# The shift's weights from POOL's queue, begun within the scale's stage, and the input transposes spread over three groups of sums

## The chip, the cores and the metric

The kernel runs on one core of one Trainium2 chip. The metric is the device time of one execution in microseconds (us), lower is better. The engines are TensorE (PE; its weight loads have a row of their own, PEld), VectorE (DVE), ScalarE (ACT), GpSimd (POOL) and SyncE (SP). SP and POOL issue the transfers spoken of here, and 16 DMA engines carry them.

## What is computed

One layer of an encoder step: a layer norm whose result is scaled and shifted by columns that come from a small vector `c`, one wide input projection, four mixer branches (state space, attention, mLSTM, convolution), an output projection and a last norm. The change lies in the first line and a half:

```
shift, scale, gate = jnp.split(c.astype(jnp.float32) @ w_mod + b_mod, 3, axis=-1)
u = layer_norm(x) * (1.0 + scale[:, None]) + shift[:, None]
# then: proj = u @ w_in, split into the inputs of the four branches
```

There are 1024 prompt rows (worked on in two halves) and 32 sample rows; the model width is 2048, which is 16 blocks `k` of 128.

## The kernel before

**Number format.** Each projection is done as three products of split operands: `u = uh + ul` and `w = wh + wl`, with matmuls `uh*wh`, `ul*wh`, `uh*wl`. The shift is not added to `uh` and `ul`; instead, each `uh`/`ul` tile has two spare columns (0 and 1) that hold the shift, and a column tile of the projection that has these columns gets its bias from them.

**The scale's stage**, `startup()` (L1384 to L1467). `load_norm` loads five row tiles of `x` (four of 128 rows, one with the 32 sample rows) and normalises them on ACT (L275). `quads(g)` brings 16 weight tiles of group g of the scale (`wmr`, 256 KB each, L1420, issued by SP) into the pool IO, which has 20 tiles, and adds them up on PE in four steps of four matmuls (L208), here called quads. With four groups there are 16 quads. After the fourth quad of a group `mod_columns` copies the sum (`mr`, DVE, L231), transposes it (`modc`, PE, L233), reduces it and writes four scale columns (DVE, L236 and L240). With these `build_u0(k)` builds four blocks of `u`: five transposes on PE (L297 and L299, here one set, tile `xt`), the scaling on ACT (L301), the split on DVE (L302, L304) and POOL (L303, 32 columns). `parts_of(g)` are four parts of 12 matmuls each (L1437 to L1439), which multiply the blocks of group g for two column tiles, "gates", that need no shift. PE's order is written out by hand (`inorder`): the parts of group g-1 stand between the builds of group g.

**The shift's stage.** Two more gate tiles (L362 to L364) are woven with `mod_group(g, 0)`, the same sums for the shift's columns: 64 loads, issued by SP at L217, one load or one quad at a time at 64 places. `shift_columns` (POOL, L287 and L288) writes the spare columns, and the first column tile with a shift follows. Weights of the column tiles are loaded by SP as well (L333).

`behind(a, b)` makes instruction a stand after b in the order, without a wait.

Of the kernel before, what the change touches and what calls it, by code (L numbers as in the profile page):

```python
# [13 lines left out]
P = 128  # L14
# [48 lines left out]
def step_kernel(ctx, tc, xp, xs, cst, wmss, wmg, bgate, win, wsm, wout, lng, lnb, ck, cv,  # L63
# [136 lines left out]
    inorder = tc.keep_in_program_order  # L200
    begun = [None]
# [9 lines left out]
    def mod_group(g, part):  # L211
        o = ZT("mod")
        for kq in range(4):
            ws = []
            for i in range(4):
                wr = IO("wmr")
                nc.sync.dma_start(wr[:, 0:512], wmss[g, 4 * kq + i, part])  # L217
                ws.append(wr)
                if i < 3:
                    yield 1  # L220
# [30 lines left out]
    def load_norm(src, rows, keep):  # L251

        tiles = []
        for q in range(4):
            if keep and q < 3:
                t = up.tile([P, 546], F32, tag=("uh", "ul")[(len(keep) + q) % 2], name=nm("x"))
            else:
                t = (IO if keep else WK)("x")
# [12 lines left out]
        if keep:  # L271
            nb = SM(1, "bnb", 3)
            V.scalar_tensor_tensor(nb[:rows], mv[:rows, 0:1], -1.0, rs[:rows], op0=ALU.mult, op1=ALU.mult)
            for q in range(4):
                A.activation(tiles[q][:rows, 0:512], tiles[q][:rows, 0:512], AF.Identity, bias=nb[:rows],  # L275
                             scale=rs[:rows])
# [13 lines left out]
    def build_u0(xts, k):  # L290

        uh, ul = new_u(0, k)
        uf = WK("uf")
        q, o = divmod(k, 4)
        pt = ST("xt")
# [4 lines left out]
        for pp, n, c0, j in ((pt, 512, 0, 0), (pt2, SMP, 512, 1)):  # L300
            A.activation(uf[:, c0:c0 + n], pp[:, 0:n], AF.Copy, scale=scale1[:, k, j:j + 1])  # L301
        V.tensor_copy(uh[:, 2:546], uf[:, 0:544])  # L302
        return (G.tensor_tensor(ul[:, 514:546], uf[:, 512:544], uh[:, 514:546].bitcast(F32), op=ALU.subtract),  # L303
                V.tensor_tensor(ul[:, 2:514], uf[:, 0:512], uh[:, 2:514].bitcast(F32), op=ALU.subtract))  # L304
# [1081 lines left out]

    def startup():
# [58 lines left out]

        m = quads(0)
        for _ in range(3):  # L1450
            next(m)
        for g in range(4):
            o = next(m)
            m = quads(g + 1) if g < 3 else iter(())
            p = parts_of(g - 1) if g else iter(())
            next(p, None)
            mod_columns(g, 1, o, inorder)
            for i in range(4):
                if i < 3:
                    next(p, None)  # L1460
                begun[1:] = build_u0(xts, 4 * g + i)
                if i < 3:
                    next(m, None)
        for _ in parts_of(3):
            pass
        for x in range(2):
            keep_gate(x, [(acc[x][i][:, 0:n], t0, n) for i, (_, t0, _, n) in enumerate(sp_)])  # L1467

    startup()
    for i in begun:  # L1470
# [36 lines left out]
    def chain(*gs):  # L1507
        for g in gs:
            yield from g

# [23 lines left out]
    for h in range(2):  # L1534
# [7 lines left out]
        if h == 0:  # L1542
            weave([(stage1(b_gate(p)), 2) for p in range(2, 4)], [(chain(*[mod_group(g, 0) for g in range(4)]), 64)])
# [126 lines left out]
```

## Time and profile before

| what | us |
|---|---|
| median of 3 runs (1965.37 to 1971.18) | 1969.03 |
| the profiled execution | 1967.32 |
| its span on the core | 1965.3 |
| PE busy within the span | 1885.7 (96%) |
| start to the first quad | 21.26 |
| the scale's stage, from there to the first matmul of L362 | 72.5 |
| from there to the first shifted column tile | 81.1 |

All times of rows are from the start of the span. A row of a timeline gives the start, the time to the end of the last of its instructions, the engine, the line, the operation with its tiles (out<-in, partitions x elements), how many instructions run on without a gap (every matmul of 32-bit operands at L208, L233 and L297 is recorded in two passes in some rows, so that a quad is x8), and in brackets the idle time ahead and what ended it. The distance from one row's start to the next row's start is the time that PE's order spends on the row. In the rows by stretch, each engine has its busy time and the number of its instructions; PEclk is the clock that PE was granted (1.00 is 2.4 GHz, 0.50 is 1.2 GHz), and behind it are the busy share of the DMA engines and what they moved. No record of the clock exists ahead of 37.7 us, so the 1.00 of the first stretch covers its later part only; the rows at L208 show two paces, 1.94 us and 1.07 us for a quad.

### The profile page before, as it was taken

What the parts mean: (1) busy time and instruction counts of PE and PEld (TensorE: products, weight loads), DVE (VectorE), ACT (ScalarE), POOL (GpSimd) and SP (SyncE); (2) the same over time, 40 slices, a digit from 0 to 9 for tenths busy, and PEclk for the clock granted to TensorE, in tenths of its full rate; (3) what the DMA queues carried; (4) which work ended last, traced back from release to release, by engine and by line L of the source; (5) the groups of instructions that cost most, each with busy time, mean ns of one, the idle gap of its engine ahead of it and who ended that gap; (6) DMA issues with size and microseconds to landing.
All of it is one profiled execution on the core that took longest, in us unless ns stands there. A gap on an engine that the chain in (4) does not pass through costs nothing. (4 is left out here: it accounts for less than half of the span.)

```text
span 1965.3 us, 31995 instructions
## 1 busy us (share of the span) xinstructions
PE 1885.7 (96%) x12162; PEld 1570.6 (80%) x12162; DVE 1343.0 (68%) x2581; ACT 774.5 (39%) x1288; POOL 320.5 (16%) x542
## 2 busy tenths in 40 slices
PE   4999999999999999999999999999999899999997
PEld 1779899998888999976788786777878676778887
DVE  5416566967866858887778869885857673356665
ACT  5213433334564334545444444533335521133321
POOL 1100111211222202441101011121112320001000
PEclk9999999999999999999999999999999999999999
DMA  9885344334443343644232332432333654467643
GB/s 346 301 305 184 102 138 131 108 123 123 142 158 123 110 126 105 166 135 133 98 104 96 116 112 78 125 110 96 129 98 113 199 153 156 135 211 259 222 134 126
DMA packets 159930, 291.42 MB, mean 148 GB/s; under 512 B 23904, under 2 KB 66144, under 8 KB 159776
## 3 DMA queue, kind: packets, MB, share of 16 engines
q1 hardware_dynamic: 156960, 280.47, 44.5%
q0 software_dynamic: 2816, 8.92, 1.2%
q8 instruction: 95, 1.56, 0.3%
q14 instruction: 59, 0.48, 0.1%
HBM read 253.50 MB, written 35.82 MB: 147 GB/s over the span
## 5 line engine op out<-in xcount | busy, mean ns | idle before, releaser
L362 PE MATMUL ip<-uh,wh 128*128 128x512 f32 (+3 forms) x2304 | 759.0, 330 | 0.9 <-POOL uh L287 0.9
L364 PE MATMUL ip<-uh,wl 128*128 128x512 f32 (+3 forms) x2304 | 745.3, 323 | 0.0
L363 PE MATMUL ip<-ul,wh 128*128 128x512 f32 (+3 forms) x2304 | 745.1, 323 | 0.1
L337 ACT CAST wh<-wr 128x1024 fp32r<-128x1024 f32 x253 | 263.9, 1044 | 624.4 <-PE ip L363 343.1
L338 DVE TENSOR_TENSOR wl<-wr,wh 128x1024 fp32r<-128x1024 f32 x253 | 313.1, 1238 | 251.3 <-ACT wh L337 222.8
L362 PEld LDWEIGHTS ip<-uh,wh 128*128 128x128 f32 x2304 | 438.9, 191 | 45.2 <-issue 14.6
L364 PEld LDWEIGHTS ip<-uh,wl 128*128 128x128 f32 x2304 | 438.1, 190 | 31.7 <-issue 1.3
L363 PEld LDWEIGHTS ip<-ul,wh 128*128 128x128 f32 x2304 | 438.6, 190 | 30.9 <-issue 2.2
L1263 PE MATMUL op<-wh,yl 128*128 128x512 f32 (+1 forms) x576 | 215.2, 374 | 0.0
L1261 PE MATMUL op<-wh,yh 128*128 128x512 f32 (+1 forms) x576 | 214.9, 373 | 0.0
L1262 PE MATMUL op<-wl,yh 128*128 128x512 f32 (+1 forms) x576 | 214.4, 372 | 0.0
L1117 DVE SCALAR_TENSOR_TENSOR cv<-cin,cs,cv 128x574 f32<-128x574 f32 (+1 forms) x240 | 187.1, 780 | 2.6
L1263 PEld LDWEIGHTS op<-wh,yl 128*128 128x128 f32 x576 | 108.5, 188 | 25.6 <-issue 6.4
L1262 PEld LDWEIGHTS op<-wl,yh 128*128 128x128 f32 x576 | 108.5, 188 | 24.1 <-issue 4.8
L1261 PEld LDWEIGHTS op<-wh,yh 128*128 128x128 f32 x576 | 108.5, 188 | 22.7 <-issue 3.1
L809 POOL TENSOR_SCALAR_AFFINE_SELECT s<-s 128x128 f32<-128x128 f32 x64 | 38.3, 599 | 416.1 <-ACT s L708 415.8
L1170 DVE SCALAR_TENSOR_TENSOR gacc<-wg,cs,gacc 128x512 f32<-128x512 f32 x120 | 92.3, 789 | 11.0 <-DMA wg<-in_wmg_dram 10.9
L208 PE MATMUL mod<-wmr,cpad 128*32 128x512 f32 x256 | 38.4, 676 | 27.4 <-DMA wmr<-in_wmss_dram 27.2
L717 DVE TENSOR_TENSOR_SCAN pr<-kp 128x128 f32<-128x128 f32 (+4 forms) x66 | 53.7, 814 | 13.0 <-POOL kp L811 10.3
L721 DVE TENSOR_TENSOR s<-s,pr 128x512 f32<-128x512 f32 (+5 forms) x106 | 59.7, 566 | 1.8
L708 ACT ACTIVATE s<-z 128x512 f32<-128x512 f32 (+3 forms) x96 | 47.6, 496 | 33.1 <-PE z L738 30.5
L1071 POOL TENSOR_TENSOR dn<-dn,mhalf 128x1 f32<-128x1 f32 (+1 forms) x36 | 27.7, 770 | 194.3 <-DVE dn L1070 190.6
(384 smaller groups left out, 2342.1 us busy)
## 6 DMA issues: line engine op xcount, KB each, us to landing
wr<-in_win_dram SPq DMA_DIRECT2D x192, 512.0 KB
wmr<-in_wmss_dram SPq DMA_DIRECT2D x128, 256.0 KB
wr<-in_wout_dram SPq DMA_DIRECT2D x63, 512.0 KB
wg<-in_wmg_dram SPq DMA_DIRECT2D x64, 256.0 KB
x<-in_xp_dram SPq DMA_DIRECT2D x32, 256.0 KB
xr<-in_xp_dram SPq DMA_DIRECT2D x28, 256.0 KB
yf<-ysc SPq DMA_DIRECT2D x16, 272.0 KB
xk<-in_xp_dram SPq DMA_DIRECT2D x16, 256.0 KB
```

The lines of the kernel that those rows point to most:

```text
L337: A.copy(wh, wr)
L338: V.tensor_tensor(wl, wr, wh.bitcast(F32), op=ALU.subtract)
L362: T.matmul(pt[:, 0:n], wh[:, k % 8, :], uh[:, c0:c0 + n], start=(k == 0), stop=False)
L363: T.matmul(pt[:, 0:n], wh[:, k % 8, :], ul[:, c0:c0 + n], start=False, stop=False)
L364: T.matmul(pt[:, 0:n], wl[:, k % 8, :], uh[:, c0:c0 + n], start=False, stop=(k == KD - 1))
L717: V.tensor_tensor_scan(pr[0:rows, 0:nk][:, ::-1], kp[0:rows, 0:nk][:, ::-1], kp[0:rows, 0:nk][:, ::-1], initial=init, op0=ALU.mult, op1=AL ...
L721: V.tensor_tensor(s[0:rows, 0:m], s[0:rows, 0:m], pr[0:rows, 1:m + 1], op=ALU.mult)
L1117: V.scalar_tensor_tensor(acc[:, 0:n], t[:, i:i + n], C("cdw", 31 * j + i), acc[:, 0:n], op0=ALU.mult, op1=ALU.add)
L1170: V.scalar_tensor_tensor(acc[j][:, 0:512], wr[:, 0:512], cT[:, k, j:j + 1], acc[j][:, 0:512], op0=ALU.mult, op1=ALU.add)
L1261: T.matmul(acc[t][:, 0:w], yh[:, c], wh, start=(first and i == 0), stop=False)
L1262: T.matmul(acc[t][:, 0:w], yh[:, c], wl, start=False, stop=False)
L1263: T.matmul(acc[t][:, 0:w], yl[:, c], wh, start=False, stop=(last and i == len(ws) - 1))
```

## The change

The transposes of x are taken out of `build_u0`. A new `turn_x(xts, k)` transposes the unscaled x into an SBUF tile `xT` (copied from PSUM by DVE or ACT). Six sets stand between the quads of the first group, five each in the next two groups, and none in the last. `build_u0` now reads `xT`: ACT scales it into `uh`, ACT, POOL and DVE do the rest. The parts of group g now follow the builds of the same group g. Half of the normalising of x goes from ACT to DVE. The loads of `mod_group` are issued by POOL instead of SP; they stand in the order behind `hold`, POOL's last instruction of the build of k = 11. Twelve of the 64 steps of the shift's sums (three quads of its first group with their twelve loads) are done within the scale's stage, ahead of the last group's quads; the other 52 stay in the weave.

```diff
 def mod_group(g, part):
-        o = ZT("mod")
+        o = ST("mod") if g == 0 else ZT("mod")
...
-                nc.sync.dma_start(wr[:, 0:512], wmss[g, 4 * kq + i, part])
+                behind(nc.gpsimd.dma_start(wr[:, 0:512], wmss[g, 4 * kq + i, part]), hold[0])
...
 def load_norm(src, rows, keep):
-                t = (IO if keep else WK)("x")
+                t = WK("x")
...
             for q in range(4):
-                A.activation(tiles[q][:rows, 0:512], tiles[q][:rows, 0:512], AF.Identity, bias=nb[:rows],
-                             scale=rs[:rows])
+                x = tiles[q][:rows, 0:512]
+                if q % 2:
+                    V.tensor_scalar(x, x, rs[:rows], nb[:rows], op0=ALU.mult, op1=ALU.add)
+                else:
+                    A.activation(x, x, AF.Identity, bias=nb[:rows], scale=rs[:rows])
...
-    def build_u0(xts, k):
-        uh, ul = new_u(0, k)
-        uf = WK("uf")
+    def turn_x(xts, k):
         q, o = divmod(k, 4)
+        xT = up.tile([P, 546], F32, tag=("uh", "ul")[k % 2], name=nm("xT")) if k < KD - 1 else IO("xT")
         pt = ST("xt")
         for t in range(4):
             inorder(T.transpose(pt[:, t * P:(t + 1) * P], xts[t][0][q][:, o * P:(o + 1) * P], ident))
         pt2 = AT("xt2")
         inorder(T.transpose(pt2[:, 0:SMP], xts[4][0][q][0:SMP, o * P:(o + 1) * P], ident[0:SMP, 0:SMP]))
-        for pp, n, c0, j in ((pt, 512, 0, 0), (pt2, SMP, 512, 1)):
-            A.activation(uf[:, c0:c0 + n], pp[:, 0:n], AF.Copy, scale=scale1[:, k, j:j + 1])
-        V.tensor_copy(uh[:, 2:546], uf[:, 0:544])
-        return (G.tensor_tensor(ul[:, 514:546], uf[:, 512:544], uh[:, 514:546].bitcast(F32), op=ALU.subtract),
-                V.tensor_tensor(ul[:, 2:514], uf[:, 0:512], uh[:, 2:514].bitcast(F32), op=ALU.subtract))
+        if k % 2:
+            A.copy(xT[:, 0:512], pt)
+        else:
+            V.tensor_copy(xT[:, 0:512], pt)
+        V.tensor_copy(xT[:, 512:544], pt2[:, 0:SMP])
+        return xT
+
+    def build_u0(xT, k):
+        uh, ul = new_u(0, k)
+        x, h = xT[:, 0:512], uh[:, 2:514]
+        A.activation(h, x, AF.Copy, scale=scale1[:, k, 0:1])
+        x2, h2 = xT[:, 512:544], uh[:, 514:546]
+        A.activation(x2, x2, AF.Copy, scale=scale1[:, k, 1:2])
+        G.tensor_copy(h2, x2)
+        return (V.scalar_tensor_tensor(ul[:, 2:514], x, scale1[:, k, 0:1], h.bitcast(F32), op0=ALU.mult, op1=ALU.subtract),
+                G.tensor_tensor(ul[:, 514:546], x2, h2.bitcast(F32), op=ALU.subtract))
...
         m = quads(0)
-        for _ in range(3):
-            next(m)
+        for n in (2, 2, 2, 0):
+            o = next(m)
+            turn(n)
+        mod_columns(0, 1, o, inorder)
         for g in range(4):
-            o = next(m)
+            for k in range(4 * g, 4 * g + 4):
+                begun[1:] = build_u0(xT[k], k)
+            if g == 2:
+                hold[0] = begun[2]
+                for _ in range(12):
+                    next(shift)
             m = quads(g + 1) if g < 3 else iter(())
-            p = parts_of(g - 1) if g else iter(())
-            next(p, None)
-            mod_columns(g, 1, o, inorder)
+            p = parts_of(g)
             for i in range(4):
-                if i < 3:
-                    next(p, None)
-                begun[1:] = build_u0(xts, 4 * g + i)
-                if i < 3:
-                    next(m, None)
-        for _ in parts_of(3):
-            pass
+                o = next(m, None)
+                if g < 2:
+                    turn(1)
+                if i != 2:
+                    next(p)
+            if g < 3:
+                mod_columns(g + 1, 1, o, inorder)
+            if g < 2:
+                turn(1)
+            next(p)
...
+    shift = chain(*[mod_group(g, 0) for g in range(4)])
     startup()
+    hold[0] = None
...
-            weave([(stage1(b_gate(p)), 2) for p in range(2, 4)], [(chain(*[mod_group(g, 0) for g in range(4)]), 64)])
+            weave([(stage1(b_gate(p)), 2) for p in range(2, 4)], [(shift, 52)])
```

Three places show what moves. A name such as `wmr_825` is one tile of a pool, and what stands in brackets is which engines' or queues' semaphores the instruction waits for: DMAHW are transfers issued by SP, DMASW those issued by POOL.

PE, before, behind the third group's `modc` (`modc_654`): the end of a part, a set of transposes of the next group, that group's next quad (`mod_723` is the scale's fourth sum), and the start of a part.

```order
L1439 MATMUL ip_276<-uh_623,wl_314 128x272
L297 MATMUL xt_679<-ident,x_159 128x128 [waits Activation_49]
L297 MATMUL xt_679<-ident,x_183 128x128
L297 MATMUL xt_679<-ident,x_207 128x128
L297 MATMUL xt_679<-ident,x_231 128x128
L299 MATMUL xt_163_684<-ident,x_255 128x32 [waits Activation_49]
L208 MATMUL mod_723<-wmr_697,cpad 32x512 [waits DMAHW4_49,PE_49]
L208 MATMUL mod_723<-wmr_691,cpad 32x512 [waits DMAHW1_49]
L208 MATMUL mod_723<-wmr_693,cpad 32x512 [waits DMAHW2_49]
L208 MATMUL mod_723<-wmr_695,cpad 32x512 [waits DMAHW3_49]
L1437 MATMUL ip_277<-uh_509,wh_319 128x272
```

PE, in the changed kernel, at the same place (behind `modc_764`): the end of a part, then the shift's first sum `mod_824`. Its first quad reads `wmr_831`, `825`, `827` and `829`.

```order
L1459 MATMUL ip_278<-ul_633,wh_319 128x272
L1460 MATMUL ip_278<-uh_632,wl_320 128x272
L209 MATMUL mod_824<-wmr_831,cpad 32x512 [waits DMASW3_49,DVE_49]
L209 MATMUL mod_824<-wmr_825,cpad 32x512 [waits DMASW0_49]
L209 MATMUL mod_824<-wmr_827,cpad 32x512 [waits DMASW1_49]
L209 MATMUL mod_824<-wmr_829,cpad 32x512 [waits DMASW2_49]
L209 MATMUL mod_824<-wmr_843,cpad 32x512 [waits DMASW7_49]
```

The third quad of `mod_824`, and behind it the first quad of the scale's fourth sum (`mod_893`) and a part:

```order
L209 MATMUL mod_824<-wmr_855,cpad 32x512 [waits DMASW3_49]
L209 MATMUL mod_824<-wmr_849,cpad 32x512 [waits DMASW0_49]
L209 MATMUL mod_824<-wmr_851,cpad 32x512 [waits DMASW1_49]
L209 MATMUL mod_824<-wmr_853,cpad 32x512 [waits DMASW2_49]
L209 MATMUL mod_893<-wmr_867,cpad 32x512 [waits DMAHW4_49]
L209 MATMUL mod_893<-wmr_861,cpad 32x512 [waits DMAHW1_49]
L209 MATMUL mod_893<-wmr_863,cpad 32x512 [waits DMAHW2_49]
L209 MATMUL mod_893<-wmr_865,cpad 32x512 [waits DMAHW3_49]
L1458 MATMUL ip_275<-uh_796,wh_472 128x272 [waits Activation_49]
L1459 MATMUL ip_275<-ul_797,wh_472 128x272 [waits DVE_49]
```

So twelve matmuls on POOL's loads have come between the part and the last group's first quad, and the transposes there are gone.

POOL, before, at the end of the scale's stage and the start of the shift's: the 32-column subtractions of the builds, then the shift's columns.

```order
L303 TENSOR_TENSOR ul_871<-uf_872,uh_870 128x32 [waits DVE_49]
L303 TENSOR_TENSOR ul_898<-uf_899,uh_897 128x32 [waits DVE_49]
L303 TENSOR_TENSOR ul_913<-uf_914,uh_912 128x32 [waits DVE_49]
L983 MEMSET v1s_5621 32x2
L1367 MEMSET m_3367_19744 128x6
L1367 MEMSET m_3378_19830 128x6
L287 CAST uh_350<-shiftH 128x2 [waits DVE_49]
L287 CAST uh_418<-shiftH 128x2
```

POOL, in the changed kernel, around `hold` (`ul_818`, k = 11): the last build of the third group and the first loads of the shift.

```order
L319 CAST uh_817<-xT_676 128x32 [waits PE_49,Activation_49]
L321 TENSOR_TENSOR ul_818<-xT_676,uh_817 128x32 [waits Pool_49]
L220 DMA wmr_825<-in_wmss_dram 128x512 [waits DMAHW2_49,DMAHW1_49]
L220 DMA wmr_827<-in_wmss_dram 128x512 [waits DMAHW7_49,DMAHW2_49]
L220 DMA wmr_829<-in_wmss_dram 128x512 [waits DMAHW3_49,DMAHW0_49]
L220 DMA wmr_831<-in_wmss_dram 128x512 [waits DMAHW5_49,DMAHW6_49,DMAHW0_49,PE_49]
L220 DMA wmr_837<-in_wmss_dram 128x512 [waits DMAHW6_49,DMAHW5_49,PE_49]
```

Behind the twelve loads the builds of the fourth group, and the loads for the fourth quad of `mod_824` (`wmr_1113` to `1119`):

```order
L319 CAST uh_982<-xT_742 128x32 [waits DVE_49,Activation_49]
L321 TENSOR_TENSOR ul_983<-xT_742,uh_982 128x32 [waits Pool_49]
L319 CAST uh_989<-xT_774 128x32 [waits DVE_49,Activation_49,Pool_49]
L321 TENSOR_TENSOR ul_990<-xT_774,uh_989 128x32 [waits Pool_49]
L220 DMA wmr_1113<-in_wmss_dram 128x512 [waits DMAHW1_49,DMAHW5_49,DMASW4_49,PE_49]
L220 DMA wmr_1115<-in_wmss_dram 128x512 [waits DMAHW2_49,DMAHW6_49,DMASW5_49,PE_49]
L220 DMA wmr_1117<-in_wmss_dram 128x512 [waits DMAHW3_49,DMAHW7_49,DMASW6_49,PE_49]
L220 DMA wmr_1119<-in_wmss_dram 128x512 [waits DMAHW0_49,DMASW7_49,PE_49]
```

POOL now issues the shift's loads between the subtractions; before, it issued none here. The casts of the shift's columns (L293 and L294), which stood behind all of it at L287 and L288, now stand between later loads, those of group 0 behind 18 further loads from `wmr_1147` on.

SP, before, at the loads of the scale's last group (the first seven of 16), each of which waits for quads of the group before it:

```order
L1420 DMA wmr_691<-in_wmss_dram 128x512 [waits DMAHW1_49,PE_49]
L1420 DMA wmr_693<-in_wmss_dram 128x512 [waits DMAHW2_49,PE_49]
L1420 DMA wmr_695<-in_wmss_dram 128x512 [waits DMAHW3_49,PE_49]
L1420 DMA wmr_697<-in_wmss_dram 128x512 [waits DMAHW4_49,PE_49]
L1420 DMA wmr_699<-in_wmss_dram 128x512 [waits DMAHW5_49,PE_49]
L1420 DMA wmr_701<-in_wmss_dram 128x512 [waits DMAHW6_49,PE_49]
L1420 DMA wmr_703<-in_wmss_dram 128x512 [waits DMAHW7_49,PE_49]
```

SP, in the changed kernel, at the same loads:

```order
L1441 DMA wmr_861<-in_wmss_dram 128x512 [waits DMAHW5_49,DMAHW1_49,PE_49]
L1441 DMA wmr_863<-in_wmss_dram 128x512 [waits DMAHW6_49,DMAHW2_49,PE_49]
L1441 DMA wmr_865<-in_wmss_dram 128x512 [waits DMAHW7_49,DMAHW3_49,PE_49]
L1441 DMA wmr_867<-in_wmss_dram 128x512 [waits DMAHW4_49,DMASW3_49,PE_49]
L1441 DMA wmr_869<-in_wmss_dram 128x512 [waits DMASW0_49,PE_49]
L1441 DMA wmr_871<-in_wmss_dram 128x512 [waits DMASW1_49,PE_49]
L1441 DMA wmr_873<-in_wmss_dram 128x512 [waits DMASW2_49,PE_49]
L1441 DMA wmr_875<-in_wmss_dram 128x512 [waits DMAHW0_49,DMASW7_49,PE_49]
```

Three of them wait for quads of the third group only. From `wmr_867` on, 13 loads go into tiles of the pool that the shift's twelve loads fill first: they wait for those loads (DMASW) and for the matmuls of `mod_824` that read them, four quad by quad, and the last (`wmr_891`) for the first quad of `mod_893`.

## Rows read from the trace of the kernel before

**Rows 1.** The page: span; busy us, share and instructions of each engine

```profile
span 1965.3 us, 31995 instructions
...
PE 1885.7 (96%) x12162; PEld 1570.6 (80%) x12162; DVE 1343.0 (68%) x2581; ACT 774.5 (39%) x1288; POOL 320.5 (16%) x542
```

**Rows 2.** Busy time by stretch: length; PE, PEld, DVE, ACT, POOL; PEclk, DMA share, GB/s

```profile
21.26:60.26 39.00, 33.30 (x205) 16.34 (x206) 16.83 (x32) 18.09 (x32) 5.48 (x8) 1.00 1.02 374
60.26:93.80 33.54, 33.15 (x247) 23.82 (x246) 13.17 (x28) 10.91 (x22) 5.58 (x11) 1.00 0.85 287
93.80:174.89 81.09, 78.75 (x594) 65.38 (x593) 29.39 (x66) 14.18 (x23) 4.76 (x34) 1.00 0.83 283
```

**Rows 3.** Timeline of PE, first group of sums: start us, us, what

```profile
21.26 1.94 PE L208 MATMUL mod<-wmr,cpad 128*32 128x512 f32 x8 [21.26 <-DMA wmr<-in_wmss_dram]
24.16 1.94 PE L208 MATMUL mod<-wmr,cpad 128*32 128x512 f32 x8 [0.97 <-DMA wmr<-in_wmss_dram]
...
29.57 1.94 PE L208 MATMUL mod<-wmr,cpad 128*32 128x512 f32 x8 [0.78 <-DMA wmr<-in_wmss_dram]
32.49 1.08 PE L233 MATMUL modc<-ident,mr 128*128 128x128 f32 x4 [0.98 <-DVE mr L231]
33.37 1.06 PE L297 MATMUL xt<-ident,x 128*128 128x128 f32 x4
```

**Rows 4.** Timeline of PE, third group of sums and after

```profile
57.33 1.07 PE L208 MATMUL mod<-wmr,cpad 128*32 128x512 f32 x8
...
58.33 0.39 PE L1437 MATMUL ip<-uh,wh 128*128 128x272 f32 x1
...
60.26 0.60 PE L233 MATMUL modc<-ident,mr 128*128 128x128 f32 x4
60.61 0.38 PE L1437 MATMUL ip<-uh,wh 128*128 128x272 f32 x1
...
62.23 0.60 PE L297 MATMUL xt<-ident,x 128*128 128x128 f32 x4
...
62.94 1.07 PE L208 MATMUL mod<-wmr,cpad 128*32 128x512 f32 x8
...
74.53 0.60 PE L233 MATMUL modc<-ident,mr 128*128 128x128 f32 x4
...
93.80 0.29 PE L362 MATMUL ip<-uh,wh 128*128 128x272 f32 x1
```

**Rows 5.** Timelines of ACT (25.73, 62.87) and DVE (61.12)

```profile
25.73 2.93 ACT L275 ACTIVATE x<-x,bnb,brs 32x512 f32<-32x512 f32 x4 [0.40 <-DVE bnb L273]
62.87 0.86 ACT L301 ACTIVATE uf<-xt,scale 128x512 f32<-128x512 f32 x2 [4.74 <-PE xt L297]
61.12 0.17 DVE L240 SCALAR_TENSOR_TENSOR scale<-mods,cs 128x8 f32<-128x8 f32 x1
```

**Rows 6.** Groups by line and form: busy us, mean ns of one, idle before

```profile
L301 ACT ACTIVATE uf<-xt,scale 128x512 f32<-128x512 f32 x16 | 11.0, 687 | 30.6 <-PE xt L297 30.6
...
L304 DVE TENSOR_TENSOR ul<-uf,uh 128x512 fp32r<-128x512 f32 x16 | 11.1, 692 | 0.5
...
L303 POOL TENSOR_TENSOR ul<-uf,uh 128x32 fp32r<-128x32 f32 x16 | 11.0, 684 | 72.4 <-DVE uh L302 72.4
...
L1282 POOL DMA_DIRECT2D rsc<-val x20 | 11.0, 550 | 168.3 <-DVE val L1277 167.8
```

**Rows 7.** DMA issues: KB each, median us from issue to landing

```profile
rsc<-val POOLq DMA_DIRECT2D x16, 256.0 KB, 4.4
...
out_dram<-val POOLq DMA_DIRECT2D x16, 256.0 KB, 4.6
...
out_dram<-val POOLq DMA_DIRECT2D x4, 64.0 KB, 3.1
```

**Rows 8.** Busy time in slices of 2 us around a stall of PE (columns as in 2)

```profile
198.00:200.00 2.00, 0.46 (x4) 0.25 (x4) 1.92 (x6) 1.98 (x2) 0.00 (x0) 1.00 0.10 20
...
202.00:204.00 2.00, 2.00 (x10) 1.63 (x10) 0.59 (x8) 0.41 (x2) 0.25 (x1) 0.50 0.32 88
```

More of the change, by code (lines that the diff above doesn't have):

```diff
@@ L200, in step_kernel @@
     inorder = tc.keep_in_program_order
+    hold = [None]
     begun = [None]
@@ L1384, in step_kernel, with chain @@
     rsc = dp.tile([5 * P, D], F32, name="rsc")
+    def chain(*gs):
+        for g in gs:
+            yield from g
     def startup():
@@ L1445, in parts_of, with turn @@
                     yield 1
+        xT = []
+        def turn(n):
+            for _ in range(n):
+                xT.append(turn_x(xts, len(xT)))
         m = quads(0)
-        for _ in range(3):
-            next(m)
+        for n in (2, 2, 2, 0):
+            o = next(m)
+            turn(n)
+        mod_columns(0, 1, o, inorder)
         for g in range(4):
-            o = next(m)
+            for k in range(4 * g, 4 * g + 4):
[4 more added lines that the diff above has]
+                    next(shift)
             m = quads(g + 1) if g < 3 else iter(())
-            p = parts_of(g - 1) if g else iter(())
-            next(p, None)
-            mod_columns(g, 1, o, inorder)
+            p = parts_of(g)
             for i in range(4):
-                if i < 3:
-                    next(p, None)
-                begun[1:] = build_u0(xts, 4 * g + i)
-                if i < 3:
-                    next(m, None)
-        for _ in parts_of(3):
-            pass
+                o = next(m, None)
[8 more added lines that the diff above has]
+            next(p)
         for x in range(2):
             keep_gate(x, [(acc[x][i][:, 0:n], t0, n) for i, (_, t0, _, n) in enumerate(sp_)])
+    shift = chain(*[mod_group(g, 0) for g in range(4)])
     startup()
+    hold[0] = None
     for i in begun:
@@ L1505, in stage1 @@
                 return
-    def chain(*gs):
-        for g in gs:
-            yield from g
     def stage_n(g, n):
```

## The prediction

> **What bounds the kernel now.** I read the page first, then the table by stretch, then PE's timeline in the first 100 us. PE is busy in 96% of the span [rows 1], so a change can win only where PE waits or runs at a low clock, and it loses wherever it makes PE wait. The change touches two stretches. The scale's stage runs from the first quad at 21.26 [rows 3] to the first column tile at 93.80 [rows 4], 72.5 us. At full pace one quad costs 1.0 us (57.33 to 58.33), one part 1.62 (60.61 to 62.23), one set of transposes 0.71 (62.23 to 62.94), one `modc` 0.35 (60.26 to 60.61) [rows 4]. So 16 quads, 16 parts, 16 sets and 4 `modc` are 16.0 + 25.9 + 11.4 + 1.4 = 54.7 us, and the stage loses 17.8. The loss lies early: PE is idle for 5.7 us of 21.26 to 60.26 but only for 0.4 us of 60.26 to 93.80 [rows 2], and the first group's quads take 1.94 us and the first set 1.47 (33.37 to 34.84, where the next quad begins) [rows 3] against 1.0 and 0.71 later, which is the low one of the clock's two levels. In the same stretch the DMA engines are full, share 1.02 at 374 GB/s [rows 2]. The shift's stage, 93.80 to 174.89, has only 81.09 - 78.75 = 2.3 us of idle PE [rows 2]. So there is something to win before 60 us and almost nothing to win behind it.
>
> **The change part by part.** All sums are made against the profiled execution, 1967.3 us, which is 1.7 below the median; at the end I add the difference to the median.
>
> (1) Transposes into the first group. The first group's quads wait 0.78 to 0.97 us each for their loads [rows 3]; six sets are put there. They need all five tiles of x. Before, ACT ends the last one at 28.66 [rows 5]; with half of the pieces on DVE I take 25. Three more quads and six sets from there are 25 + 3 x 1.94 + 6 x 1.47 = 39.6 at the low level and 25 + 3 x 1.0 + 6 x 0.71 = 32.3 at the high one. Before, the high level came some 16 us after the first quad, behind gaps; with fewer gaps I take it as coming earlier, and 35 for the end of the group.
>
> (2) To the third group's `modc`, which I call T0. PE has eight quads (8.0), nine sets (6.4), seven parts (11.3) and two `modc` (0.7): 26.4. To it come waits: `mr` 0.98 [rows 3]; behind the first scale the builds of group 0 with nothing but a quad and a set to cover them, about 2.5; 0.8 for the rest. T0 is 35 + 26.4 + 4.3, or about 66, with 63 to 70 from the ends of (1). Before it was 60.26 [rows 4], but three parts and eight sets less had been done by then (10.5 us). So parts (1) and (2) win some 5 us. The third group's quads can't be much earlier than before, at 57 [rows 4], since they follow loads that ran on full DMA engines [rows 2].
>
> (3) The new wait. PE's order now has the shift's first quad right behind one `modc`, one set and one part, 2.7 us after T0. Its loads can be issued only behind POOL's last instruction of k = 11. Counted from T0: the scale is there at +1.03 (61.29 less 60.26 [rows 4, 5]); ACT does a copy of the last set (0.69, by the row of 512 at L301) and four pairs of 0.86 [rows 5, 6], to +5.2; POOL's cast and subtraction, at most 0.68 each [rows 6] and of them some 1.0 after ACT's end, to +6.2. Four issues of 0.55 [rows 6] put the fourth load's issue at +7.9. The trace has no load by POOL. Its stores land 3.1 us (64 KB) to 4.6 us (256 KB) after their issue [rows 7]; I take 4.4, the lower of the two rows of the same size, so that the quad runs at about +12. PE, out of work at +2.7, is idle for about 9 us (8 at 3.1). Nothing covers it: all later matmuls stand behind it in PE's order.
>
> By the Trainium skill ("DMA: Bandwidth & Descriptors", Anatomy of one DMA — SWDGE (gpsimd) path) a transfer by POOL's path takes about 2.0 us and its bytes at 436 GB/s; for 256 KB this would be an estimate of 2.6 us, below the rows' 3.1 to 4.6, and the wait would be some 2 us less. No run here shows it yet.
>
> (4) The last group's quads. Thirteen of its loads go into tiles that the shift's twelve fill first, so 25 loads of 256 KB follow one another, 6.55 MB, 17.5 us at 374 GB/s [rows 2]. Counted from +8.5, when the first can arrive, the last is there at about +26, and with quad and copy the fourth `modc` stands at about +28.5; before, it came at +14.3 (74.53 less 60.26 [rows 4]). In between PE has only three shift quads, four quads and three parts (11.9 us of work): the rest is idle or low-level time. The clock falls in such a place: in the slice from 198 PE was busy for 0.46 of 2.0 us, and two slices on PEclk is 0.50 [rows 8]. As long as loads set the pace it costs nothing; it adds up to 4 us if the quads do.
>
> The same pages ("DMA: Bandwidth & Descriptors", Issuing engines are not separate DMA queues) say that transfers of several issuing engines share the same 16 DMA engines and only issue time is saved. That speaks against this part: the second queue brings no bandwidth, and with full engines in rows 2 the trace agrees.
>
> (5) To the column tiles. After that `modc` come the scale, four pairs on ACT, DVE's subtraction (0.69), and four parts of which the first can start at about +34; the fourth ends at +40.5. Into it the order puts the shift's fourth quad; its loads stand on POOL behind k = 15, so they are issued from about +34.3 and land at +40.9. With the quad the first column tile starts at +43, that is 66 + 43 = 109. Before, it started at 93.80 [rows 4] without any of the shift's quads; four of them are 4.0 us. So this stretch is longer by 109.3 - 97.8 = 11.5 us.
>
> (6) The shift's stage. Twelve quads less one after another, loads by POOL. Casts that wait for DVE now stand between loads, but behind 18 loads that are more than a whole group ahead, so I count 0. Bounds: all of the idle 2.3 gone [rows 2], or one whole issue of four and landing, 2.2 + 4.4 = 6.6, not covered [rows 6, 7]. SP's queue of weight loads gets shorter; PE doesn't wait for it there. Half of the normalising on DVE, the SBUF tile and the other split on ACT, DVE and POOL lie beside PE's work, since all are below 55% busy in each stretch [rows 2]; where they do not, it is counted in (2) and (3).
>
> Sum: +11.5 us on 1967.3, or about 1979 for a profiled execution and 1980.5 beside the median of 1969.0. Its own range: -2.5 from (1) and (2), -3 from two shorter landings, -2 from (6) give 1973; +4 from (1) and (2), +4 from the clock and part of (6) give 1990.
>
> **The rivals.** *The start becomes dense and pays for the wait.* If the clock rises soon after the transposes begin, PE follows the loads: the third group's last quad would come at 57, as before, and T0 at 58.5. With short landings the column tiles then start at 58.5 + 43 - 3 = 98.5 against 97.8, and with (6) at its lower end the sum is -1.5 us: no change, or slightly faster. If also the 25 loads arrive in less than 17.5 us (issue alone would allow 13.8, 25 x 0.55), it is -5, 1964. It decides for "not slower" from T0 below about 58. For it: 17.8 us are lost and sets of transposes are there to fill the gaps. Against it: the loads were at full share already, and the new wait is bounded below by the rows at about 8.
>
> *POOL's single queue rules the shift's stage.* Three times a group's loads stand behind casts that wait for DVE; if each shows 3 to 6 us of the 6.6, the stage is 10 to 15 us longer: 1990 to 1995. Against it: 18 loads of lead.
>
> *The sample tile is late.* If the normalised sample rows come at 28.7 as before, PE's first quads stand behind the first transposes and T0 is 2 to 4 us later: 1983 to 1985, inside the forecast's range.
>
> *The order is not what the words say.* It could be that the loads, though begun earlier in the program, start no earlier than before. In PE's and POOL's order they do stand before the fourth group, so I give this no share.
>
> **How the numbers follow.** About 0.3%, 6 us, is what a measurement of this kernel can tell from no change. The forecast (with the late sample tile in it) has 0.62, POOL's queue in the shift's stage 0.12, the dense start 0.26, of which 0.16 falls within 6 us of the time before and 0.10 below. So slower 0.73 (the forecast's lowest end falls just within 0.3%, which takes 0.01), same 0.17, faster 0.10. The likeliest is the forecast, 1980.5. The range from 1966 to 1991 leaves out most of the faster cases and the worst of POOL's queue.
>
> **What would show it.** In the profile after: PE's wait in front of the shift's first quad, 8 to 10 us long and ended by a transfer, at about 69 us; the third `modc` near 66 and the fourth near 94; the first quad that waits for transposes near 25; the granted clock at 0.50 somewhere between 70 and 95; the first matmul of the two woven gates near 109; and no more than 3 us of idle PE behind it up to the first shifted tile. The prediction is wrong if POOL's loads land well before 3 us, if T0 is below 60, or if the last group's quads follow the shift's within 5 us.

## The result: 1.1% slower, by some 21 us

| | before | after |
|---|---|---|
| median of the runs, us | 1970.11 (1965.37 to 1973.55) | 1990.49 (1989.30 to 1993.35) |
| the profiled execution's span, us | 1965.3 | 1987.0 |
| third `modc` begins, us | 60.26 | 64.33 |
| fourth `modc` begins, us | 74.53 | 94.19 |
| the woven gates begin, us | 93.80 | 112.18 |

The ratio is 1.0107, with a 95% interval of 1.0082 to 1.0132. The forecast had the direction and 1980.5; the loss is nearly twice the 11.5 us of its sum.

The page of the changed kernel, with the lines that answer to [rows 1] and, last, the quads with the time that PE waited ahead of them (before, the page had 27.4 us there; some 21 us of either figure are the time ahead of the very first quad):

```profile
span 1987.0 us, 32086 instructions
...
PE 1890.7 (95%) x12162; PEld 1572.1 (79%) x12162; DVE 1350.1 (68%) x2599; ACT 772.1 (39%) x1286; POOL 357.2 (18%) x622
...
L209 PE MATMUL mod<-wmr,cpad 128*32 128x512 f32 x256 | 37.9, 672 | 41.5 <-DVE bst L268 21.0
```

The table by stretch, cut at the third `modc`, the fourth, the first gate and the 201st `uh*wh` matmul of the kernel, which in both kernels stands behind the last of the shift's sums (64 of the 200 ahead of it are in the parts). The columns are those of [rows 2]:

```profile
21.02:64.33 43.31, 39.31 (x264) 22.71 (x265) 23.86 (x53) 18.01 (x33) 7.03 (x16) 1.00 0.85 314
64.33:94.19 29.86, 18.19 (x116) 8.78 (x114) 4.25 (x8) 4.46 (x10) 9.52 (x20) 0.77 0.76 276
94.19:112.18 17.99, 13.63 (x74) 10.88 (x73) 7.03 (x15) 7.25 (x14) 9.98 (x21) 0.81 0.51 170
112.18:187.84 75.66, 69.79 (x522) 57.46 (x521) 28.34 (x63) 13.25 (x22) 26.04 (x76) 0.98 0.80 286
```

The last row's counterpart in the kernel before, to the same matmul (201st):

```profile
93.80:165.72 71.92, 69.58 (x523) 56.21 (x521) 23.87 (x55) 11.81 (x19) 4.76 (x34) 1.00 0.84 290
```

The 201st matmul comes at 187.84 instead of 165.72, 22.1 us later; from there to the end of the span the two kernels need 1799.1 and 1799.6 us. So in these two executions the whole loss lies in front of it. PE is idle for 11.7 us of 64.33 to 94.19 and for 4.4 us of the 18 us behind, at both levels of the clock in each, and for 5.9 us of the last stretch where the kernel before has 2.3.

PE's timeline around the early steps:

```profile
64.33 0.60 PE L236 MATMUL modc<-ident,mr 128*128 128x128 f32 x4
...
66.98 0.29 PE L1460 MATMUL ip<-uh,wl 128*128 128x272 f32 x1
76.81 1.93 PE L209 MATMUL mod<-wmr,cpad 128*32 128x512 f32 x8 [9.53 <-DMA wmr<-in_wmss_dram]
80.12 1.94 PE L209 MATMUL mod<-wmr,cpad 128*32 128x512 f32 x8 [1.39 <-DMA wmr<-in_wmss_dram]
82.81 3.41 PE L209 MATMUL mod<-wmr,cpad 128*32 128x512 f32 x16 [0.75 <-DMA wmr<-in_wmss_dram]
...
90.57 2.06 PE L209 MATMUL mod<-wmr,cpad 128*32 128x512 f32 x16
...
110.06 1.06 PE L209 MATMUL mod<-wmr,cpad 128*32 128x512 f32 x8 [2.17 <-DMA wmr<-in_wmss_dram]
```

And POOL's, whose loads (L220) stand behind the builds' casts and subtractions (L319, L321), which wait for ACT, which in its turn needs the scale of the group's `modc`:

```profile
70.27 0.24 POOL L321 TENSOR_TENSOR ul<-xT,uh 128x32 fp32r<-128x32 f32 x1
70.84 0.74 POOL L220 DMA_DIRECT2D wmr<-in_wmss_dram  x1 [0.33 <-issue]
71.73 6.00 POOL L220 DMA_DIRECT2D wmr<-in_wmss_dram  x11 [0.15 <-issue]
96.87 0.58 POOL L319 CAST uh<-xT 128x32 fp32r<-128x32 f32 x1 [19.13 <-ACT xT L318]
...
100.59 0.24 POOL L321 TENSOR_TENSOR ul<-xT,uh 128x32 fp32r<-128x32 f32 x1
101.16 5.45 POOL L220 DMA_DIRECT2D wmr<-in_wmss_dram  x10 [0.33 <-issue]
```

Between 77.7 and 101.2 POOL issues nothing. What that does to the DMA engines stands in the same table, cut finer (columns as above):

```profile
67.30:76.81 9.51, 0.00 (x1) 0.04 (x2) 2.26 (x3) 2.06 (x6) 8.47 (x18) 0.76 0.45 145
76.81:86.15 9.34, 7.20 (x33) 1.00 (x33) 0.00 (x0) 0.00 (x0) 0.79 (x2) 0.52 1.02 378
86.15:94.19 8.04, 8.04 (x65) 5.23 (x61) 0.69 (x1) 0.58 (x1) 0.00 (x0) 1.00 0.97 361
94.19:100.00 5.81, 4.14 (x26) 3.08 (x24) 2.61 (x5) 4.33 (x9) 2.33 (x6) 0.96 0.01 3
100.00:106.30 6.30, 5.79 (x22) 5.16 (x23) 3.50 (x8) 1.49 (x3) 5.73 (x13) 0.50 0.52 135
```

From 76.81 to 94.19 the DMA engines are full, and PE waits for them until the quads at 82.81; from 94.19 to 100 they move 3 GB/s, since POOL has nothing to issue.

In the kernel before, SP issued the first of these loads at 68.73 and 18 of them by 83.9:

```profile
68.73 15.18 SPq L217 DMA_DIRECT2D wmr<-in_wmss_dram  x18
```

So the loads that the change begins earlier in the program begin 2.1 us later on the chip (70.84), and the thirteenth is issued at 101.16.

### The profile page after: what moved, and what is told of

Read it like the earlier page. It is cut to its first block, busy times and chain, and to the rows that moved or that the text cites. A ratio compares the mean times of both kernels' runs of the same rounds, so it can differ in the third digit from the quotient of the medians.

```text
span 1987.0 us, 32086 instructions
## 1 busy us (share of the span) xinstructions
PE 1890.7 (95%) x12162; PEld 1572.1 (79%) x12162; DVE 1350.1 (68%) x2599; ACT 772.1 (39%) x1286; POOL 357.2 (18%) x622
```

## The experiments

A first set asks which part costs: the early steps' place on PE, POOL's queue, or the new build. Ratios are against the kernel before, measured beside each set (its medians lay between 1970.1 and 1972.7 us). Where two runs are compared and their intervals overlap, the text says so.

**Without early steps (e1).** The twelve early `next(shift)` are out; the loads stay on POOL.

```diff
-            if g == 2:
-                hold[0] = begun[2]
-                for _ in range(12):
-                    next(shift)
...
-[(shift, 52)]
+[(shift, 64)]
```

> The changed kernel without its twelve early steps: all 64 steps of the shift's sums stand in the weave, its loads stay on POOL's queue. Theory (the place costs: PE's order holds the last group's quads behind quads whose loads POOL can issue only after k = 11, and those loads take the tiles of the last group's): the 9.5 us wait near 67 us goes, the fourth modc comes at some 77 us instead of 94, the gates begin before 94, and the time falls to 1966 to 1973. Rival (POOL's queue itself is slow, wherever the steps stand): the shift's quads wait in the weave what they waited before, and the time stays above 1982.

Measured: 1989.92 us, 1.0093 (1.0075 to 1.0111). The theory falls. The wait at 67 us is gone and the fourth `modc` comes at 78.23, but the loss is the same: the loads now start only behind k = 15 and are held up again by the casts of the shift's columns, which wait for DVE, as POOL's timeline shows,

```profile
84.10 0.24 POOL L321 TENSOR_TENSOR ul<-xT,uh 128x32 fp32r<-128x32 f32 x1
84.71 5.56 POOL L220 DMA_DIRECT2D wmr<-in_wmss_dram  x10 [0.36 <-issue]
...
118.81 1.49 POOL L293 CAST uh<-shiftH 128x2 fp32r<-128x2 f32 x4 [5.77 <-DVE shiftH L248]
120.24 0.54 POOL L220 DMA_DIRECT2D wmr<-in_wmss_dram  x1
```

and PE waits 10.0 us in front of the shift's quads.

**The same with the loads on SP (e2),** so that only the spread transposes and the new build remain.

```diff
-behind(nc.gpsimd.dma_start(wr[:, 0:512], wmss[g, 4 * kq + i, part]), hold[0])
+nc.sync.dma_start(wr[:, 0:512], wmss[g, 4 * kq + i, part])
```

> The changed kernel without early steps and with the shift's loads issued by SP as before the change: what stays is the spreading of the transposes and the new build. Theory: the third modc at 64 us as in the changed kernel, with three parts and eight sets more done than before, some 6 us ahead; about 3 us are given back at the builds of the last group, which nothing covers; 1963 to 1968, that is 1 to 6 us faster than before. Rival (the new build costs more on DVE, ACT and POOL than it gives): 1970 to 1976.

Measured: 1970.82 us, 1.0004 (0.9987 to 1.0021). The third `modc` is at 64.53, 3.9 us ahead (4.3 us later than before, with two parts and seven sets, 8.2 us, more done), and the total wins nothing: no gain as in the theory, and a time at the low end of the rival's range. Part of the lead goes at the last builds: the gates are at 90.12 with two of the shift's quads done (before: 93.80 and four), 1.7 us ahead at equal work. The rest goes in the weave, whose 201st `uh*wh` matmul is 2.2 us late (167.96). There SP's queue waits 24.4 us for DVE ahead of weight loads (before: 18.4), and 80 to 95 us moves 189 GB/s (before: 241); that this is what costs is argued, not shown.

**Only the queue (e3).** In the kernel before, the one word of the shift's load:

```diff
-                nc.sync.dma_start(wr[:, 0:512], wmss[g, 4 * kq + i, part])
+                nc.gpsimd.dma_start(wr[:, 0:512], wmss[g, 4 * kq + i, part])
```

> The kernel before with one word changed: the shift's loads are issued by POOL instead of SP; its transposes, builds and order are the old ones. Theory (POOL's line, with builds and casts in it, is the loss, and neither the spread transposes nor the early steps are): the loads start behind the last build, near 90 us, the casts hold later ones, and the time is 1982 to 1992. Rival (the queue hurts only together with the new order): 1969 to 1976.

Measured: 1986.05 us, 1.0072 (1.0046 to 1.0097). One word makes two thirds of the loss. POOL's first load is at 86.17, behind the last subtraction, where SP had issued its first at 68.73, and later loads stand behind the casts:

```profile
85.47 0.75 POOL L303 TENSOR_TENSOR ul<-uf,uh 128x32 fp32r<-128x32 f32 x1 [0.38 <-DVE uh L302]
86.17 5.54 POOL L217 DMA_DIRECT2D wmr<-in_wmss_dram  x10
...
116.79 1.54 POOL L287 CAST uh<-shiftH 128x2 fp32r<-128x2 f32 x4 [4.82 <-DVE shiftH L245]
```

**Early steps, loads on SP (e4):** the changed kernel with the edit of e2.

> The changed kernel with its early steps at their place on PE, but all loads of the shift issued by SP, behind nothing. Theory (the wait comes from the issue behind k = 11, the rest from the shared tiles): the first early quad finds its data, the 9.5 us wait falls below 2, but the last group's loads still follow the shift's quads, so the fourth modc comes some 4 to 8 us later than without early steps; 1966 to 1974. Rival (the place alone costs, whichever queue issues): still above 1980.

Measured: 1974.41 us, 1.0026 (1.0011 to 1.0040), at the upper end of the theory's range: no wait before the first early quad (67.74), the fourth `modc` at 84.87 against 76.86 in e2. So of the changed kernel's loss POOL's queue is some 16 us. The place costs some 4 us by the medians of e4 and e2; their intervals overlap.

**Early on POOL, the other 52 on SP (e5):** `nc.sync` wherever `hold[0]` is None.

> The changed kernel with the twelve early loads on POOL's queue as they are, and the other 52 steps' loads issued by SP. Theory (POOL's queue in the shift's stage costs the 3.8 us by which that stage is longer): the waits before quads in the weave fall from 5.8 us to about 1, and the time falls by some 4 us, to 1985 to 1988. Rival (that stage is longer for another reason, such as DVE's or ACT's work that has moved into it): the same time as the changed kernel, 1989 to 1992.

Measured: 1986.02 us, 1.0076 (1.0057 to 1.0095). This fits the theory: PE's waits before quads behind the gates fall from 5.8 to 2.5 us, and the time by 4.5, though the interval overlaps with that of the changed kernel.

A second set asks why POOL's queue costs: by what stands in its line, or by its transfers.

**POOL freed (e7):** e1 with these four instructions on DVE.

```diff
-        G.tensor_copy(uh[:, 0:2], shiftH[:, k, :].bitcast(F32))
-        G.tensor_copy(ul[:, 0:2], shiftL[:, k, :].bitcast(F32))
+        V.tensor_copy(uh[:, 0:2], shiftH[:, k, :].bitcast(F32))
+        V.tensor_copy(ul[:, 0:2], shiftL[:, k, :].bitcast(F32))
...
-        G.tensor_copy(h2, x2)
+        V.tensor_copy(h2, x2)
...
-                G.tensor_tensor(ul[:, 514:546], x2, h2.bitcast(F32), op=ALU.subtract))
+                V.tensor_tensor(ul[:, 514:546], x2, h2.bitcast(F32), op=ALU.subtract))
```

> The run without early steps and with the loads on POOL (e1), but POOL freed of all other work in these stages: the 32-column cast and subtraction of the builds and the casts of the shift's columns go to DVE. Theory (POOL's loads are late only because they stand in one line with work that waits for ACT and DVE): the first shift load is issued by 70 us instead of 84.7, no stretch between 64 and 150 us moves less than 230 GB/s, and the time is 1968 to 1974. Rival (transfers by POOL's path are slow by themselves, 5.9 us to landing): the waits before the shift's quads stay, the time is above 1983.

Measured: 1967.42 us, 0.9993 (0.9973 to 1.0013). The whole loss of e1 is gone with the queue unchanged. The first load is at 72.39 (later than expected, but 12 us ahead of e1). That trace is of an execution 14 us above the median, but nearly all of this lies behind the shift's stage: its 201st `uh*wh` matmul is at 166.99, e1's at 181.87. This settles it for the kernel without early steps: the line costs, not the transfers.

**Only the casts on DVE (e8).**

> The run without early steps and with the loads on POOL (e1), with the casts of the shift's columns on DVE; the builds' 32-column work stays on POOL. Theory (two places hold POOL's loads up, the last builds at the start and the casts in the weave, about half of the loss each): loads still start at 84 to 85 us, but the waits of POOL for DVE (26.4 us) are gone and the time is 1976 to 1983. Rival (transfers by POOL's path are slow by themselves): 1988 to 1991.

Measured: 1977.74 us, 1.0036 (1.0019 to 1.0053). Of e1's loss the casts make about 12 us and the builds 10, by intervals (of e1, e8 and e7) that do not overlap.

**POOL freed, with early steps (e9):** the changed kernel with the edit of e7.

> The changed kernel with its early steps at their place and the loads on POOL, with POOL freed of the builds' 32-column work and of the casts (both on DVE), and the first loads thus behind nothing of POOL that waits for the third scale. Theory: the loads start before 66 us, PE's wait before the first early quad falls from 9.5 us to below 2, and what stays is the last group's loads behind the shift's, as with SP as the issuer (1974): 1970 to 1977. Rival (transfers by POOL's path are slow by themselves): above 1983.

Measured: 1981.25 us, 1.0058 (1.0039 to 1.0078), worse than the theory and short of the rival. The early quads no longer wait, but the last group's do, since POOL now issues the next loads beside them. PE at the last quad of the last group, in e9 and below it in e4:

```profile
88.05 1.94 PE L209 MATMUL mod<-wmr,cpad 128*32 128x512 f32 x8 [5.50 <-DMA wmr<-in_wmss_dram]
```

```profile
81.46 1.06 PE L209 MATMUL mod<-wmr,cpad 128*32 128x512 f32 x8 [2.69 <-DMA wmr<-in_wmss_dram]
```

A reading of these two rows: in one queue (e4) the loads that PE needs first go first; in two they share the engines, which are full in both (393 GB/s in e9 from 80 to 92, 396 in e4 from 77 to 85). But most of e9's time does not go here: with its gates at 107.39 its 201st `uh*wh` matmul comes at 171.56, only 5.8 us later than before, and the other 10 us of this trace's 16.2 are lost behind it, where the changed kernel lost none. What costs there stays open.

**The other 52 held (e15):** as e9, but the builds of k = 12 to 15 stay on POOL.

```diff
+        E = V if k < 12 else G
-        V.tensor_copy(h2, x2)
+        E.tensor_copy(h2, x2)
...
-                V.tensor_tensor(ul[:, 514:546], x2, h2.bitcast(F32), op=ALU.subtract))
+                E.tensor_tensor(ul[:, 514:546], x2, h2.bitcast(F32), op=ALU.subtract))
```

> The changed kernel with the casts and the 32-column work of the builds of k = 0 to 11 on DVE; that of k = 12 to 15 stays on POOL. So the twelve early loads stand behind no work that waits for the third scale, but the other 52 stand behind the last builds as in the changed kernel, and PE's order is that of the changed kernel. Theory (in e9, at 1981, the later loads of POOL's queue shared the engines with the last group's loads and held these up): PE's wait before the first early quad falls below 2 us as in e9, the last group's quads come at the pace of e4, the fourth modc below 89 us, and the time is 1974 to 1979. Rival (the late start of the 52 costs as much as the sharing did): 1980 to 1986.

Measured: 1981.35 us, 1.0050 (1.0031 to 1.0069). The fourth `modc` is at 88.48 instead of 92.15, as the theory had it; the time is the rival's. The 52 now start at 95.28, and 80 to 95 moves 134 GB/s; that their late start costs just what sharing did is argued from the equal times.

**Builds alone on DVE (e14), casts alone (e12, again e13, first half of the rows only e16).**

> The changed kernel with the 32-column work of all builds on DVE; the casts of the shift's columns stay on POOL between the loads. Theory (the builds' place in POOL's line is the larger part of the loss and the casts add some 3 to 10 us in the weave): 1983 to 1989. Rival (the casts cost nothing, by the run with only them moved): 1980 to 1982, as with both moved.

> The changed kernel with the casts of the shift's columns on DVE; the builds' work stays on POOL ahead of the early loads. Theory (of the 21 us the start, up to the first woven gate, has 18 and the casts have what is left): the start is as in the changed kernel and the time is 1984 to 1988. Rival (without the casts POOL makes up for the late start, as it did without early steps, where they were 12 us): 1976 to 1981.

> The run with the casts on DVE (e12) once more, with more rounds, since its time (1991.7) and its trace (3 us less than the changed kernel by the end of the shift's stage) spoke against one another. Theory (the casts hold loads for 3 us, later work hid it by chance): 1985 to 1989. Rival (the casts cost nothing where the start is early): 1989 to 1993.

> The run with the casts on DVE (e13), but for the first half of the rows only; in the second half, which builds its blocks long after this stage, the casts stay on POOL as in the changed kernel. Theory (the casts hold loads for 5 to 7 us of the weave, and casts on DVE in the second half cost about as much later): 1984 to 1988. Rival (the casts' loss in the weave is no loss to the end): 1989 to 1993.

Measured: the builds 1987.77 us, 1.0076 (1.0054 to 1.0097); the casts 1.0104 (1.0079 to 1.0130), 1.0098 (1.0077 to 1.0120) and 1.0092 (1.0066 to 1.0117), or 1991.73, 1991.96 and 1990.12 us. Moved alone, the builds are some 6 us of the changed kernel's loss and the casts 3 us at most, by intervals that overlap with that of the changed kernel. With the casts moved already (e12, 1.0104, against e9, 1.0058) the builds are 9 us, by intervals that do not overlap. The theories of e12, e13 and e16 are not borne out. In these traces the weave was about 6 us shorter (69.16 us in e16 against 75.66) but began 2 to 6 us later, and executions differ by as much at the first group's quads; how much is the casts' stays open.

**The clock (e6).** Sixty transposes of the identity fill PE's wait.

```diff
             if g == 2:
                 hold[0] = begun[2]
+                pw = AT("warm")
+                for _ in range(60):
+                    inorder(T.transpose(pw[:, 0:P], ident, ident))
```

> The changed kernel with 60 transposes of the identity, which nothing reads, in PE's order ahead of the first early quad, about 8 of the 9.5 us in which PE waits there; nothing else is changed. Theory (the low clock of 67 to 86 us costs nothing, since loads set the pace there): the clock is at its high level when the early quads begin, and the time stays within 1988 to 1992. Rival (the low clock is a part of the loss): the fourth modc comes 3 us earlier or more and the time is 1984 to 1987.

Measured: 1990.59 us, 1.0100 (1.0077 to 1.0124). The first quad runs at the high level, the next one not, and both wait as before:

```profile
69.65 6.71 PE L1487 MATMUL warm<-ident 128*128 128x128 f32 x60
80.48 1.07 PE L209 MATMUL mod<-wmr,cpad 128*32 128x512 f32 x8 [4.12 <-DMA wmr<-in_wmss_dram]
83.02 1.93 PE L209 MATMUL mod<-wmr,cpad 128*32 128x512 f32 x8 [1.47 <-DMA wmr<-in_wmss_dram]
87.58 3.64 PE L209 MATMUL mod<-wmr,cpad 128*32 128x512 f32 x16 [2.63 <-DMA wmr<-in_wmss_dram]
```

So filling the wait buys nothing. What the low clock itself costs is not settled by it, since the later quads ran at the low level here as well: in the changed kernel the two quads from 82.81 took 3.41 us where two at the high level take 2.06 (90.57), and PE had no gap from there to the fourth `modc`, which makes at most 1.4 us.

A third set looks for a better kernel. **e10** takes e2 and puts twelve steps between the last group's parts; **e11** does this to e7; **e17** and **e18** are e7 and e11 with the casts on DVE for the first half of the rows only.

```diff
             for i in range(4):
+                if g == 3:
+                    for _ in range(3):
+                        next(shift)
                 o = next(m, None)
...
+        E = V if h == 0 else G
-        V.tensor_copy(uh[:, 0:2], shiftH[:, k, :].bitcast(F32))
+        E.tensor_copy(uh[:, 0:2], shiftH[:, k, :].bitcast(F32))
```

> The spread transposes, the shift's loads issued by SP, and twelve steps of the shift's sums between the four parts of the last group (three to a part), the other 52 in the weave. Theory (spread transposes win 5 us by the third modc and give them back in that the shift's last quads come late in the weave; begun earlier, behind the last group's quads, they give less back): 1964 to 1969. Rival (the loads' rate sets the end of the weave whatever the order): 1969 to 1973.

> The same order as in the run before this one (e10), with the loads on POOL's queue and POOL freed of the builds' and the casts' work, which DVE does. Theory (a line of its own for these loads is worth a little, since weight loads that wait for DVE no longer stand ahead of them): 1962 to 1968. Rival (the loads of POOL's line take bandwidth from the weight loads and the last group's loads that PE waits for): 1969 to 1976.

> The run with POOL freed and no early steps (e7, 1967.4), the casts on DVE in the first half only. Theory (casts on DVE in the second half cost some 4 us): 1961 to 1966, faster than before. Rival (they cost nothing): 1966 to 1970.

> The run with POOL freed and twelve steps between the last group's parts (e11, 1968.1, whose shift stage ended 2.6 us earlier than that of the kernel before), the casts on DVE in the first half only. Theory: 1960 to 1965, faster than before. Rival: 1966 to 1970.

Measured: e10 1973.35 us, 1.0013 (0.9998 to 1.0029), the rival's side; e11 1968.08, 0.9988 (0.9974 to 1.0003); e17 1966.96, 0.9971 (0.9955 to 0.9986); e18 1965.89, 0.9975 (0.9962 to 0.9989), beside 1970.29 for the kernel before. By their ratios the last two are faster than both kernels, than the kernel before by some 5 us (3 to 4 by the medians), though not by what was expected; since their intervals overlap with e7's, it isn't shown that the second half's casts made the difference. The table by stretch of e17, 64 to 110 us (its trace, at 1969.80, is the slowest of its executions):

```profile
64.00:80.00 16.00, 15.80 (x117) 10.52 (x117) 6.70 (x20) 6.58 (x12) 5.56 (x10) 1.00 0.89 329
80.00:95.00 15.00, 14.01 (x105) 8.99 (x103) 7.17 (x21) 4.41 (x10) 10.60 (x20) 1.00 1.00 375
95.00:110.00 15.00, 14.73 (x113) 10.20 (x106) 2.52 (x3) 2.01 (x4) 7.77 (x16) 1.00 1.03 400
```

and of e1, the same queue with the builds in its line:

```profile
64.00:80.00 16.00, 15.81 (x119) 11.61 (x118) 5.75 (x13) 6.61 (x12) 2.97 (x8) 1.00 0.64 217
80.00:95.00 15.00, 10.24 (x47) 8.21 (x49) 5.76 (x11) 5.01 (x12) 9.28 (x20) 0.73 0.55 192
```

## Why the prediction was right in direction and short by half

**Steps (1) and (2), T0: right; what it was compared with, wrong.** 64.33 against 66. The first sets wait for the sample tile until 25.05, as assumed, and from 26.10 on quads take 1.06 us; the first group's `modc` comes at 33.5, where 35 was taken for the group's end. But ahead of its own third `modc` the kernel before has two parts and seven sets less (5 and 8 in its trace, 7 and 15 in the other), not three and eight: 8.2 us, not 10.5. So the start was 4.1 us ahead at T0; that this is near the 5 us of the prediction is luck.

**Step (3), the wait: right.** 9.53 us against 9, and the first early quad at +12.5 against +12. The fourth load was issued 0.6 us later than assumed and landed sooner (a median of 3.3 us for the four, 3.1 for the first, against 4.4): two small misses that cancel. The Trainium skill's figure ("DMA: Bandwidth & Descriptors", Anatomy of one DMA — SWDGE (gpsimd) path), an estimate of 2.6 us, was below every median seen here.

**Step (4): right in size, in part by another path.** Fourth `modc` at +29.9 against +28.5. The loads set the pace only up to the quads at 82.81 (+18.5); from there PE runs without a gap on its own work. Of the low clock's price, at most 1.4 us, see e6. The rule of the same pages of the Trainium skill (Issuing engines are not separate DMA queues) held: e9's two queues moved no more than e4's one (393 and 396 GB/s).

**Step (5): this is where it failed.** The 4.0 us that were credited for four of the shift's quads were no gain. The prediction said that the kernel before starts its gates "without any of the shift's quads". Its timeline says otherwise; behind the fourth `modc` (74.53), when all 16 quads of the scale are done, there are four more quads, which can only be the shift's:

```profile
78.65 1.07 PE L208 MATMUL mod<-wmr,cpad 128*32 128x512 f32 x8
82.42 1.06 PE L208 MATMUL mod<-wmr,cpad 128*32 128x512 f32 x8
86.15 1.06 PE L208 MATMUL mod<-wmr,cpad 128*32 128x512 f32 x8
89.63 1.06 PE L208 MATMUL mod<-wmr,cpad 128*32 128x512 f32 x8
```

So at equal work the gates are 112.18 - 93.80 = 18.4 us late, not 11.5: 4.0 from the credit, 2.9 because the gates start at 112.18 instead of 109.3. These 2.9 are the 3.5 us by which the chain from the fourth `modc` to the gates was longer (18.0 instead of 14.5), less small misses ahead of it. Counted from that `modc`, the fourth quad's loads were issued at +7.0 instead of +5.8 and had landed at +15.9 instead of +12.4: the six loads issued from 101 us on took 6.5 us to land in the median, where 4.4 was taken. The clock was at 0.50 from 100 to 106.3, but this lies in front of PE's 2.17 us wait for those loads and is covered by it. The same four quads lower the 17.8 us that the prediction found lost in the old scale's stage to 13.8. And the early steps brought nothing earlier: the kernel before had done as many shift quads by its gates, and had begun their loads 2.1 us sooner. The rival that was given no share, that the loads start no earlier than before, was true.

**Step (6): mis-sized.** 0 was taken, with 6.6 as the upper bound; it was 3.7 (75.66 against 71.92), of which e5 shows that it goes with POOL's queue, by intervals that overlap. The reason given, 18 loads of lead ahead of the casts, counted order and not time: the thirteenth load is issued at 101.16. That this is the reason is argued; the casts alone are not shown to cost here (e12, e13, e16).

With 11.5, 4.0, 2.9 and 3.7 the sum comes to the 22.1 us by which the 201st matmul is late.

**The cause.** The prediction placed the loss in PE's order and in the shared tiles. e1, e3 and e7 show that without that order the same queue loses as much or two thirds of it, and that with POOL freed of compute it loses nothing. In the changed kernel e4 shows some 16 of the 20 us to go with POOL's queue; e9 shows about half of the loss to go with POOL's builds and casts, and e12 against e9 the builds to be the larger part. The rest of the queue's share, some 7 us between e9 and e4 (whose intervals just touch), stays open: sharing and the late start are two readings that e15 could only exchange, and in e9's trace most of its loss arises behind the shift's stage. **The rivals:** POOL's queue ruling the shift's stage was nearest in size (1990), though its mechanism, the casts, is not borne out there, and that stage gave only 3.7 us. The start became denser, but not below the 58 us of that rival, and e2 shows that it pays for nothing by itself.

## What to carry to other kernels

Before moving loads to an engine's queue, list the compute that stands in front of them on that engine and what this waits for: the same queue with and without such compute was 23 us apart (e1 and e17). Look up when the loads start now, before calling a new place early. And when two orders are compared at a milestone, count on both sides the work that is already done there, in the trace and not in the program text.

## What was not expected of the hardware

The transfers of POOL's queue took 5.8 us in the median from issue to landing in the changed kernel, but 3.1 for the first, when the DMA engines were nearly idle, and 6.5 for the six from 101 us on; in these rows the landing time went with how full the engines were, and it is not by itself a loss (e7 has the same queue and none). Filling PE's wait with transposes kept the clock up for the first quad behind it (1.07 us) and no longer (1.93 us for the next; 0.57 from 80 to 92 in e6).
